# Six modulation vectors of the first layer: from TensorE to VectorE, and later in the mixer

## The chip, the core and the metric

The kernel runs on one core of a Trainium2 chip. Its metric is the device time of one execution, in microseconds. A core has TensorE (PE, with PEld for its weight loads), VectorE (DVE), ScalarE (ACT), GpSimd (POOL) and SyncE (SP), which issues the DMAs; each takes its instructions strictly in the order in which they were written for it.

## The reference, cut to what matters

Two layers run over 256 latent and 256 context tokens of width 1024. Each begins with the modulation, `mod = split(silu(c) @ w_mod + b_mod, 6)`, once for `c` and once for `c_ctx`; the two share the weights, and each of the six vectors of a layer needs a 1024x1024 matrix (4 MB in fp32). Then:

```
h  = modulate(rmsnorm(x), mod[0], mod[1])      # latent and context tokens
ys = differential attention(h), hyena convolution(h), windowed attention(h)
x  = x + mod[2] * ((sum_b sigmoid(gate_b) * (ys[b] @ w_branch[b])) @ w_out)
h2 = modulate(rmsnorm(x), mod[3], mod[4])
x  = x + mod[5] * expert_choice_moe(h2)        # router top 32 of 256 tokens, 16 experts
```

In the second layer the context tokens are only read. The vectors 2 to 5 of the first layer are thus needed at the end of its mixer at the earliest (5 only in its mixture of experts), and 0 and 1 of the second layer at that layer's start.

## The kernel before, in words

The mixer of a layer is a list of output blocks. A block is 128 columns of a projection for all 512 tokens: over eight slices k of the contraction it does three matmuls `mm3` (high and low halves of fp32 operands, so as to keep fp32 precision), 24 matmuls 128x512 into one bank. Its weights come by DMA as `wraw`; ScalarE rounds them to `wh`, and VectorE and GpSimd each form half of the rest, `wl = wraw - wh`. The first layer has 116 blocks: 0 to 23 for the eight differential heads, 24 to 47 for the hyena columns, 48 to 51 the first of the windowed attention (SWA), 52 to 107 the pairs of gate and branch for the three branches (with eight SWA blocks among the first of them), and 108 to 115 for `w_out`. Before a branch begins, the tasks whose output it reads must be finished (`drain`), and their sum is split into halves `yb`.

All else is a background task: a generator that issues a few instructions at a time between the slices k of the blocks (`Background.pump`, l. 366). Such groups are `filter` (the hyena filter), `diff` (a differential head), `hy` (a channel group of the hyena convolution: forward transform, product with `K`, inverse transform), `swa` and the modulation. Which instruction comes next is settled while the program is written down, by a cost model of the engines (`Model`, l. 144): a step is taken when its inputs are expected to be ready, a credit that grows with TensorE's time allows it, and ScalarE and VectorE aren't expected to be more than 1.5 us behind (`BACKLOG`). A group in `LAZY` stands at the end of the live tasks from when it is added, and so takes only what the others leave.

The vectors 0 and 1 of the first layer are computed before block 0. What the change touches is the rest:

- `mod_run` (l. 707) takes TensorE: for each k it loads 512 KB (`wm`, a whole row block of a vector's matrix) and issues four matmuls 32x256 in four column tiles of one bank, with both streams' `sc` as the small operand. I call these four matmuls of one k a round; a profile counts eight records for one. `mod_out` turns the result and adds the bias.
- `run` (l. 1948) adds group `modN` ahead of the mixer: vectors 2, 3, 4 of layer 0 and 0, 1 of layer 1, 40 rounds. Group `modA` is added after block 112 (l. 1555) for vector 5 of layer 0, 8 rounds, and is drained in the MoE after the first selection of tokens (l. 1887).
- `mod_vec` (l. 727) takes VectorE, and serves the second layer's vectors 3 to 5: an accumulator `ma` of 1024 columns, one operation `ma = wm * sc + ma` (scalar_tensor_tensor, STT) for each k, and at the end eight records of matmuls with a column selector, which sum over the partitions. In the second layer it is added `MODR` = 58 blocks ahead of the mixer's last.
- `pre_out` (l. 1535) drains `mod` and `modN` before block 108.

After the mixer come the routing (norm, router, selection of 32 tokens by expert) and the 16 experts, whose weights stream in by DMA.

Of the kernel before, what the change touches and what calls it, by code (L numbers as in the profile page):

```python
# [32 lines left out]
RATE = (0.75, 0.6)  # L33
LOW = (4, 3)
FAST = 1.5
COST = {"setup": 500.0, "filter": 60000.0, "mod": 15000.0, "modA": 5000.0, "modN": 5000.0, "diff": 9000.0, "hy": 10000.0, "swa": 4000.0, "post": 1000.0}
CREDIT = (3000.0, 4000.0)
SLACK = 200.0
LATER = (6, 4)
# [2 lines left out]
FILTER_E = 4  # L42
SIDE = 2
LAZY = ("mod",)
MODR = 58
PREF = ({7: 1, 6: 2, 5: 3, 4: 4}, {28: 1, 22: 2, 7: 3, 4: 4, 3: 5})
HD = 64
NH = 8
# [359 lines left out]
class Kernel:  # L408
# [295 lines left out]
        self.nc.sync.dma_start(t, self.A["w_mod"][l, k * 128:(k + 1) * 128, v * D:(v + 1) * D])  # L704
        return t

    def mod_run(self, vs, depth, pause, delay=3000.0):
        todo = [(l, v, k) for l, v in vs for k in range(KT)]
        raw = deque(self.mod_load(*todo.pop(0)) for _ in range(depth))
        yield wait(raw[0], delay=delay)  # L710
        for l, v in vs:
            acc = self.bank([128, 256], "m")
            for k in range(KT):
                w = raw.popleft()
                for c in range(4):
                    self.mm(acc[c * 32:(c + 1) * 32, :], self.sc[:, k, :], w[:, c * 256:(c + 1) * 256], k == 0, k == KT - 1, 4)
                w = None
                if todo:
                    yield wait(gate=self.room(a4=1))
                if todo:  # L720
                    raw.append(self.mod_load(*todo.pop(0)))
                yield wait(*list(raw)[:1], delay=pause)
            yield wait(acc, bank=0)
            yield from self.mod_out(l, v, acc)
            yield from self.mod_post(l, v)

    def mod_vec(self, vs):
        for l, v in vs:
            n = 2 if l == 0 or v < 2 else 1
            yield wait(gate=self.room(a4=n + 2), bank=0)  # L730
            acc = [self.sb("a4", [128, D], name="ma") for _ in range(n)]
            w = self.mod_load(l, v, 0)
            for k in range(KT):
                yield wait(w, *acc, gate=self.room(a4=1), bank=0)
                nx = self.mod_load(l, v, k + 1) if k < KT - 1 else None
                for s in range(n):
                    sc = self.sc[:, k, s:s + 1]
                    if k:
                        self.stt(acc[s], w, sc, acc[s], OP.mult, OP.add)
                    else:  # L740
                        self.ts(acc[s], w, sc, None, OP.mult)
                w, nx = nx, None
            yield wait(*acc)
            p = self.bank([128, 256], "m")
            for s in range(n):
                for c in range(4):
                    self.mm(p[c * 32:(c + 1) * 32, :], self.sel[s], acc[s][:, c * 256:(c + 1) * 256], s == 0, s == n - 1, 4)
            acc = None
            yield wait(p, bank=0)
            yield from self.mod_out(l, v, p, 30)  # L750
            yield from self.mod_post(l, v)

    def mod_post(self, l, v):
# [230 lines left out]
    def run_blocks(self, bl, ahead=2, first=3):  # L984
        nl = ns = first
        later = []
        for j, b in enumerate(bl):
            self.bg.due, end = [], self.bg.now
            for c in bl[j:]:
                if c.drains:  # L990
                    self.bg.due.append((c.drains, end))
                end += 24 * (4.0 + 0.41 * c.n)
            while ns < min(max(j + ahead, first + (j > 0)), len(bl)):
                self.split_block(bl[ns], later if j else None)
                ns += 1
            while nl < len(bl) and (nl <= ns or (nl - ns < 3 and self.model.dead("a4", BUFS["a4"]) > SPARE[self.bg.layer])):
                self.load_block(bl[nl])
                nl += 1
            if self.bg.layer and len(bl) - 1 - j == MODR:
                self.bg.add("mod", lambda task: self.mod_vec([(1, v) for v in range(3, 6)]))  # L1000
            if j < first:
                while later:
                    later.pop(0)()
                if j == 0:
                    for c in bl[:first]:
                        if c.pre:
                            c.pre()
                    hi, lo = b.hl()
                    ps = [self.bank([128, c.n], "d" if i < 2 else "b") for i, c in enumerate(bl[:first])]
                    for k in range(KT):  # L1010
                        self.bg.until([hi[:, k], lo[:, k]])
                        for c, p in zip(bl, ps):
                            self.mm3(p, (c.wh[:, k], c.wl[:, k]), (hi[:, k, 0:c.n], lo[:, k, 0:c.n]), k == 0, k == KT - 1)
                b.wh = b.wl = None
                b.evac(ps[j])
                continue
            if b.pre:
                b.pre()
            hi, lo = b.hl()[:2]
            p = self.bank([128, b.n], "d")  # L1020
            for k in range(KT):
                self.bg.until([b.wh[:, k], b.wl[:, k], hi[:, k], lo[:, k]])
                self.mm3(p, (b.wh[:, k], b.wl[:, k]), (hi[:, k, 0:b.n], lo[:, k, 0:b.n]), k == 0, k == KT - 1)
                if k >= LATER[self.bg.layer] and later:
                    later.pop(0)()
                if k > LATER[self.bg.layer] and nl < len(bl) and nl - ns < 3 and self.model.dead("a4", BUFS["a4"]) > SPARE[self.bg.layer]:
                    self.load_block(bl[nl])
                    nl += 1
                if k < KT - 1:
                    self.bg.pump()  # L1030
            b.wh = b.wl = None
            if len(bl) - 1 - j in PREF[self.bg.layer]:
                self.fill(PREF[self.bg.layer][len(bl) - 1 - j])
            b.evac(p)
            self.bg.pump()
# [335 lines left out]
    def mixer(self, l):  # L1371
# [163 lines left out]
        def pre_out():  # L1535
            halve(KT - 1)
            self.bg.drain("mod")
            self.bg.drain("modN")
            self.bg.arena = None
            self.post_start(l, nq)  # L1540

# [10 lines left out]
        for j in range(KT):  # L1552
            def ev_o(p, j=j):
# [1 line left out]
                    sl = slice(s * 256, s * 256 + 256)  # L1555
                    self.stt(self.xT[:, j, sl], p[:, sl], self.modc[l][:, 2, j, s:s + 1], self.xT[:, j, sl], OP.mult, OP.add)
                self.bg.add("post", lambda task, j=j: self.post(l, j, nq))
                if j == 4 and full:
                    vs = [(l, 5)]
                    self.bg.add("modA", lambda task: self.mod_run(vs, 2, 1300.0, 19000.0 if full else 11000.0))  # L1560
            add(cols(A["w_out"][l], j * 128), lambda: self.mg, nt, ev_o, pre_out if j == 0 else None)
        return bl

# [36 lines left out]
    def moe(self, l):  # L1600
# [61 lines left out]
        def body():  # L1662
# [221 lines left out]
            room = full  # L1884
            fill(room, 1)
            select(0)
            self.bg.drain("modA")
            fill(room, 2)
            finish(gather(0))
            for g in range(1, 4):  # L1890
# [57 lines left out]
    def run(self):  # L1948
        bl = self.mixer(0)
        self.setup(bl)  # L1950
        self.bg.add("modN", lambda task: self.mod_run([(0, 2), (0, 3), (0, 4), (1, 0), (1, 1)], 1, 6000.0))
        for l in range(L):
            if l:
                self.new_arena(3)
# [40 lines left out]
```

## Time and profile before

| | |
|---|---|
| time, three runs | 2637.61 us median, 2637.21 to 2639.09 |
| profiled execution | 2639.09 us, span 2637.3 us, so 1.8 us outside the span |
| busy in the span | PE 2244.6 (85%), DVE 1332.7 (51%), ACT 883.4 (33%), POOL 786.9 (30%) |
| chain that ended last | PE 40%, DMA 16%, DVE 13% |
| first layer's blocks start (us) | 3: 61.5; 23: 236.7; 43: 437.5; 54: 565.9; 78: 777.8; 98: 900.5; 115: 1000.2 |

The block starts are the times of each block's first matmul in the trace. By them I cut the first mixer into stretches, which the rest speaks of: A (blocks 3 to 22, 61.5 to 236.7), B (23 to 42, to 437.5), C (43 to 53, to 565.9), D1 (54 to 77, to 777.75), D2 (78 to 97, to 900.5), E (98 to 115, to 1006.9), then the routing (to 1031.3). A busy share is an average over such a stretch; what a task costs the stretch depends on which engine ends last there.

### The profile page before, as it was taken

Reading aid. Unit: us, or ns where it says so; the run is one execution under the profiler, and the core shown is the slowest. Engines: PE = TensorE matmul, PEld = TensorE weight load, DVE = VectorE, ACT = ScalarE, POOL = GpSimd, SP = SyncE. Lnnn points to the kernel's source line nnn. Section 1 sums busy time; section 2 is a strip of 40 time slices with the busy share of each in tenths; the row PEclk is TensorE's granted clock in tenths of the full one; section 3 lists DMA queues with packets and bytes.
Section 4 is the critical chain, followed back from the end, with each engine's and each line's share of the span. In section 5 each row is a group of like instructions: output and inputs, shape, how many; then the busy total and the mean of one; then the engine's idle time right before and its main releaser. Section 6 shows DMA issues by size and latency. Waiting matters only on the chain.

```text
span 2637.3 us, 38629 instructions
## 1 busy us (share of the span) xinstructions
PE 2244.6 (85%) x14938; PEld 1534.3 (58%) x14938; DVE 1332.7 (51%) x2899; ACT 883.4 (33%) x1933; POOL 786.9 (30%) x775
## 2 busy tenths in 40 slices
PE   6999998889989998898989799898888987666565
PEld 4777776767768774333333277787777863232223
DVE  4777788867662324223342158778788541111111
ACT  4445653345552332101110056553554430000001
POOL 2654225642333440001110055446554630000000
PEclk8999998989999999999999999998899988777888
DMA  8433342111213377999999942242365889999998
GB/s 293 119 120 112 96 128 89 52 53 52 69 57 88 92 251 288 373 407 400 356 379 403 404 158 80 72 121 80 100 180 160 253 308 409 409 409 409 409 409 305
DMA packets 390239, 590.31 MB, mean 224 GB/s; under 512 B 45948, under 2 KB 278056, under 8 KB 388776
## 3 DMA queue, kind: packets, MB, share of 16 engines
q1 hardware_dynamic: 390056, 587.84, 62.6%
q8 instruction: 118, 1.93, 0.3%
q14 instruction: 65, 0.53, 0.1%
HBM read 584.66 MB, written 3.15 MB: 223 GB/s over the span
## 4 chain that ended last, share of the span: by engine, by line
PE 40%; DMA 16%; DVE 13%; issue 3%; ACT 2%; SPq 2%; POOL 1%; ACTq 0%; DVEq 0%; POOLq 0%
PE p L457 38%; DMA mw<-in_moe_w_dram 15%; DVE t L260 3%; DVE arena L260 3%; PE p L468 2%; SPq L260 2%; DVE wl L260 2%; DVE qp L260 1%; DVE yb L260 1%; ACT wh L260 1%; ACT arena L260 1%; DVE ma L260 0%; DMA wraw<-in_w_in_dram 0%; DVE s L260 0%; DVE aT L260 0%
## 5 line engine op out<-in xcount | busy, mean ns | idle before, releaser
L457 PE MATMUL p<-mw,xg 128*32 128x256 f32 (+1 forms) x3072 | 406.7, 514 | 120.2 <-DMA mw<-in_moe_w_dram 120.0
L457 PE MATMUL p<-hhi,wh 128*128 128x512 f32 (+1 forms) x1344 | 496.7, 370 | 11.1 <-DVE arena L260 8.2
L457 PE MATMUL p<-hhi,wl 128*128 128x512 f32 (+1 forms) x1344 | 481.4, 358 | 26.9 <-DVE wl L260 26.4
L457 PE MATMUL p<-hlo,wh 128*128 128x512 f32 (+1 forms) x1344 | 476.6, 355 | 2.5 <-POOL hlo L260 1.4
L260 POOL TENSOR_TENSOR wl<-wraw,wh 128x512 fp32r<-128x512 f32 x232 | 330.9, 1427 | 460.2 <-ACT wh L260 365.9
L457 PEld LDWEIGHTS p<-mw,xg 128*32 128x32 f32 (+1 forms) x3072 | 137.3, 132 | 331.7 <-issue 203.7
L457 PEld LDWEIGHTS p<-hhi,wl 128*128 128x128 f32 x1344 | 258.3, 192 | 76.6 <-DVE wl L260 41.8
L457 PEld LDWEIGHTS p<-hhi,wh 128*128 128x128 f32 x1344 | 259.0, 193 | 49.3 <-issue 17.7
L457 PEld LDWEIGHTS p<-hlo,wh 128*128 128x128 f32 x1344 | 259.2, 193 | 30.3 <-POOL hlo L260 2.0
L260 ACT ACTIVATE wh<-wraw 128x1024 fp32r<-128x1024 f32 x232 | 242.1, 1053 | 43.2 <-PE p L457 12.1
L457 PE MATMUL p<-mw,aT 128*32 128x256 f32 (+3 forms) x1760 | 204.0, 483 | 59.3 <-DMA mw<-in_moe_w_dram 42.4
L260 DVE TENSOR_TENSOR wl<-wraw,wh 128x512 fp32r<-128x512 f32 x231 | 195.5, 846 | 60.1 <-ACT wh L260 58.9
L260 ACT ACTIVATE arena<-p 128x512 f32<-128x512 f32 (+1 forms) x212 | 106.0, 504 | 344.7 <-PE p L457 286.2
L260 ACT ACTIVATE yS<-p 32x256 f32<-32x256 f32 (+2 forms) x84 | 35.2, 419 | 499.3 <-PE p L457 465.8
L457 PE MATMUL p<-yb,wh 128*128 128x512 f32 (+1 forms) x768 | 197.1, 347 | 0.0
L260 POOL TENSOR_TENSOR sq<-sq,sq 128x512 f32<-128x512 f32 (+1 forms) x6 | 6.4, 1058 | 577.3 <-ACT sq L260 575.4
L457 PEld LDWEIGHTS p<-mw,aT 128*32 128x32 f32 (+1 forms) x1760 | 78.0, 134 | 167.9 <-issue 86.5
L260 DVE TENSOR_TENSOR s<-s,p 128x512 f32<-128x512 f32 (+1 forms) x32 | 17.7, 554 | 290.2 <-PE p L457 290.1
L260 DVE COPY yS<-p 32x512 f32<-32x512 f32 (+1 forms) x60 | 33.3, 556 | 244.5 <-ACT yS L260 244.5
L457 PE MATMUL p<-yb,wl 128*128 128x512 f32 (+1 forms) x384 | 133.2, 347 | 17.4 <-DVE wl L260 16.3
L457 PEld LDWEIGHTS p<-yb,wh 128*128 128x128 f32 x768 | 133.3, 195 | 15.0 <-issue 1.2
L260 ACT ACTIVATE arena<-p,t 128x512 f32<-128x512 f32 (+1 forms) x192 | 116.3, 612 | 65.2 <-DVE t L260 59.2
(235 smaller groups left out, 3506.0 us busy)
## 6 DMA issues: line engine op xcount, KB each, us to landing
mw<-in_moe_w_dram SPq DMA_DIRECT2D x173, 2048.0 KB, 19.3
wraw<-in_w_in_dram SPq DMA_DIRECT2D x152, 512.0 KB, 4.0
wm<-in_w_mod_dram SPq DMA_DIRECT2D x72, 512.0 KB, 4.5
mw<-in_moe_w_dram SPq DMA_DIRECT2D x40, 512.0 KB, 15.8
mw<-in_moe_w_dram SPq DMA_DIRECT2D x17, 1024.0 KB, 21.4
wraw<-in_w_branch_dram SPq DMA_DIRECT2D x32, 512.0 KB, 3.9
wm<-in_w_mod_dram SPq DMA_DIRECT2D x5, 2048.0 KB, 8.1
wraw<-in_w_in_dram SPq DMA_DIRECT2D x32, 256.0 KB, 3.3
```

The costliest lines, as they stand in the source:

```text
L260: return f(*args, **kw)
L457: self.nc.tensor.matmul(out, lhsT=lhsT, rhs=rhs, start=start, stop=stop, skip_group_check=tiles > 1)
L468: self.nc.tensor.transpose(out, in_, self.ident[:n, :n])
```

## The change

The six vectors of `modN` and `modA` go to one new `LAZY` task, `mod_both`, which is added 62 blocks ahead of the last one, at block 53 of the first layer. It halves the columns: for each vector and half, eight loads of 256 KB, two ahead; for each k and each of the two streams one VectorE operation of 128x512 (the first a plain product, the other seven STT), so 24 products and 168 STT in all; then four matmuls 32x256 with the selectors (48 in all). `mod_run` and the groups `modN` and `modA` go. The second layer keeps `mod_vec` and 58.

```diff
-MODR = 58
+MODR = (62, 58)
...
+    def mod_both(self, vs):
+        for l, v in vs:
+            p = None
+            for hf in range(2):
+                def load(k):
+                    t = self.sb("a2", [128, 512], name="wm")
+                    self.nc.sync.dma_start(t, self.A["w_mod"][l, k * 128:(k + 1) * 128, v * D + hf * 512:v * D + hf * 512 + 512])
+                    return t
+
+                yield wait(gate=self.room(a4=1, a2=3), bank=0)
+                acc = self.sb("a4", [128, 2, 512], name="ma")
+                ws = deque(load(k) for k in range(2))
+                for k in range(KT):
+                    yield wait(ws[0], acc, bank=0)
+                    w = ws.popleft()
+                    for s in range(2):
+                        sc = self.sc[:, k, s:s + 1]
+                        if k:
+                            self.stt(acc[:, s], w, sc, acc[:, s], OP.mult, OP.add)
+                        else:
+                            self.ts(acc[:, s], w, sc, None, OP.mult)
+                    w = None
+                    if k < KT - 2:
+                        yield wait(gate=self.room(a2=1), bank=0)
+                        ws.append(load(k + 2))
+                yield wait(acc)
+                if hf == 0:
+                    p = self.bank([128, 256], "m")
+                for s in range(2):
+                    for c in range(2):
+                        q = hf * 2 + c
+                        self.mm(p[q * 32:(q + 1) * 32, :], self.sel[s], acc[:, s, c * 256:(c + 1) * 256], s == 0, s == 1, 4)
+                acc = None
+            yield wait(p, bank=0)
+            yield from self.mod_out(l, v, p, 30)
+            p = None
             yield from self.mod_post(l, v)
...
-            if self.bg.layer and len(bl) - 1 - j == MODR:
-                self.bg.add("mod", lambda task: self.mod_vec([(1, v) for v in range(3, 6)]))
+            if len(bl) - 1 - j == MODR[self.bg.layer]:
+                vs = [(1, v) for v in range(3, 6)] if self.bg.layer else [(0, v) for v in range(2, 6)] + [(1, 0), (1, 1)]
+                self.bg.add("mod", lambda task: (self.mod_vec if self.bg.layer else self.mod_both)(vs))
...
             self.bg.drain("mod")
-            self.bg.drain("modN")
...
-                if j == 4 and full:
-                    vs = [(l, 5)]
-                    self.bg.add("modA", lambda task: self.mod_run(vs, 2, 1300.0, 19000.0 if full else 11000.0))
...
-            self.bg.drain("modA")
...
-        self.bg.add("modN", lambda task: self.mod_run([(0, 2), (0, 3), (0, 4), (1, 0), (1, 1)], 1, 6000.0))
```

Since each task's steps depend on what else is waiting, the written order moves too. Counted by blocks, before and after: the eight hyena tasks' forward transforms stand 2 in B and 6 in C, and then 5 and 3; their inverses 1 and 7, then 3 and 5. Of the 32 SWA tasks, C, D1 and D2 hold 4, 24 and 4, and then none, 22 and 10. Differential rows in A and B are 12 and 22, then 11 and 23; one of the filter's eight sections in A goes to B. The STT of the new task stand 96 in D1 and 72 in D2, its first products 14 and 10, its matmuls 24 and 24; the rounds of `modN` stood 17 in A, 21 in B and 2 in C. Behind block 115 nothing differs on any engine but the loss of `modA`.

Three places show it. The first is TensorE in block 3, where before put its first round; `p_108` is the block's bank, `wm_97` the loaded matrix rows:

```order
L457 MATMUL p_108_539<-hhi_66_337,wl_102_520 128x512
L457 MATMUL p_108_539<-hhi_66_337,wh_101_519 128x512
L457 MATMUL p_108_539<-hlo_67_338,wh_101_519 128x512
L457 MATMUL p_108_539<-hhi_66_337,wl_102_520 128x512
L457 MATMUL p_118_586<-wm_97_435,sc_22_121 32x256 x4
L468 MATMUL p_120_593<-cst_1_68,arena_10_88 128x128 x4
L457 MATMUL p_108_539<-hhi_66_337,wh_101_519 128x512
L457 MATMUL p_108_539<-hlo_67_338,wh_101_519 128x512
```

and after (the block's bank is now `p_107`):

```order
L457 MATMUL p_107_537<-hhi_66_337,wl_101_518 128x512
L457 MATMUL p_107_537<-hhi_66_337,wh_100_517 128x512
L457 MATMUL p_107_537<-hlo_67_338,wh_100_517 128x512
L457 MATMUL p_107_537<-hhi_66_337,wl_101_518 128x512
L468 MATMUL p_117_584<-cst_1_68,arena_10_88 128x128 x4
L457 MATMUL p_107_537<-hhi_66_337,wh_100_517 128x512
```

The round is gone, and the transposes of the filter task (`arena_10`) follow the block's matmuls directly. The second place is VectorE in block 64, one of the branch pairs of D1, around the `wl` of block 65 (`wl_1075` before, `wl_1003` after); `sk` and `t` with `sink` belong to SWA tasks. Before:

```order
L260 TENSOR_TENSOR wl_1055_5959<-wraw_1018_5713,wh_1054_5958 128x512
L260 STREAM_SHUFFLE sh_1072_6082<-sk_1071_6080 128x256
L260 TENSOR_TENSOR sk_1071_6080<-sk_1071_6080,cst_1_68 128x256
L260 COPY arena_117_576<-p_1073_6088 128x256
L260 COPY arena_117_576<-p_1078_6108 128x128
L260 TENSOR_TENSOR wl_1075_6092<-wraw_1034_5817,wh_1074_6091 128x512
L260 TENSOR_TENSOR wl_1082_6140<-wraw_1043_5871,wh_1081_6139 128x512
L260 SCALAR_TENSOR_TENSOR arena_9_87<-arena_9_87,p_1083_6143 128x512
```

and after:

```order
L260 TENSOR_TENSOR t_1015_5688<-t_1015_5688,nsink_82_409 128x2
L260 TENSOR_TENSOR t_1015_5688<-t_1015_5688,sink_81_408 128x2
L260 TENSOR_TENSOR qp_988_5537<-arena_114_572,qp_988_5537 64x128 x2
L260 SCALAR_TENSOR_TENSOR ma_1010_5673<-wm_1012_5676,sc_22_121,ma_1010_5673 128x512 x2
L260 TENSOR_TENSOR wl_1003_5622<-wraw_975_5466,wh_1002_5621 128x512
L260 SCALAR_TENSOR_TENSOR ma_1010_5673<-wm_1013_5680,sc_22_121,ma_1010_5673 128x512 x2
L260 COPY arena_114_572<-p_1018_5719 128x512
L260 SCALAR_TENSOR_TENSOR ma_1010_5673<-wm_1017_5717,sc_22_121,ma_1010_5673 128x512 x2
```

Between SWA's steps stand two STT of one k for each pair of rows of `ma`, directly ahead of the block's `wl` and behind it. The third place is TensorE at the end of the mixer and in the routing: `mg` with `wl` is the last block's last matmul, `xT` and `lg` are the router's, `aff` the affinities. Before:

```order
L457 MATMUL p_1430_8716<-mg_1320_7867,wl_1425_8668 128x512
L457 MATMUL p_1434_8760<-wm_1416_8614,sc_22_121 32x256 x4
L468 MATMUL p_1436_8767<-cst_1_68,xT_1371_8327 128x128 x4
L457 MATMUL p_1379_8371<-xT_1371_8327,gw_544_2974 16x256 x2
L457 MATMUL p_1434_8760<-wm_1417_8616,sc_22_121 32x256 x4
L1671 MATMUL p_1451_8816<-cst_1_68,lg_1439_8780 128x16 x2
L1671 MATMUL p_1452_8817<-cst_1_68,lg_1439_8780 128x16 x2
L457 MATMUL p_1434_8760<-wm_1435_8765,sc_22_121 32x256 x4
L457 MATMUL p_1434_8760<-wm_1454_8833,sc_22_121 32x256 x4
L457 MATMUL p_1434_8760<-wm_1455_8839,sc_22_121 32x256 x4
L457 MATMUL p_1434_8760<-wm_1456_8845,sc_22_121 32x256 x4
L457 MATMUL p_1434_8760<-wm_1457_8851,sc_22_121 32x256 x4
```

and after:

```order
L457 MATMUL p_1499_8924<-mg_1386_8053,wl_1494_8876 128x512
L468 MATMUL p_1503_8968<-cst_1_68,xT_1442_8539 128x128 x4
L457 MATMUL p_1450_8583<-xT_1442_8539,gw_1135_6446 16x256 x2
L1686 MATMUL p_1518_9013<-cst_1_68,lg_1506_8981 128x16 x2
L1686 MATMUL p_1519_9014<-cst_1_68,lg_1506_8981 128x16 x2
L468 MATMUL p_1521_9030<-cst_1_68,aff_76_403 32x128 x2
```

The rounds of `modA` stood between the router's instructions, and are gone; the router's own keep their order.

## Rows read from the trace of the kernel before

**Rows 1.** The page's second part: busy tenths in 40 slices of the span.
```profile
PE   6999998889989998898989799898888987666565
...
DVE  4777788867662324223342158778788541111111
```

**Rows 2.** Busy time by stretch: PE, PEld, DVE, ACT, POOL, clock, DMA share, GB/s.
```profile
61.50:236.70 175.20, 168.98 (x920) 126.54 (x920) 134.77 (x307) 83.83 (x184) 107.86 (x136) 1.00 0.41 120
236.70:437.50 200.80, 184.99 (x1059) 141.96 (x1058) 157.32 (x368) 105.55 (x255) 60.07 (x61) 0.97 0.36 111
437.50:565.90 128.40, 106.09 (x550) 85.47 (x549) 106.02 (x159) 53.12 (x98) 78.02 (x61) 0.91 0.18 50
565.90:777.75 211.85, 201.06 (x1173) 152.60 (x1172) 140.97 (x366) 106.34 (x258) 63.02 (x75) 0.98 0.22 60
777.75:900.50 122.75, 118.84 (x569) 96.32 (x569) 44.86 (x81) 37.39 (x64) 52.45 (x34) 1.00 0.30 87
900.50:1006.90 106.40, 106.40 (x489) 84.61 (x487) 30.33 (x50) 39.51 (x97) 42.07 (x30) 1.00 0.61 207
1006.90:1031.30 24.40, 15.93 (x192) 11.39 (x191) 17.57 (x66) 5.77 (x21) 1.15 (x1) 0.79 0.89 345
```

**Rows 3.** The same view of tile wm on PE alone: PE, clock, DMA.
```profile
61.50:236.70 175.20, 10.86 (x136) 1.00 0.41 120
236.70:437.50 200.80, 13.42 (x168) 0.97 0.36 111
437.50:565.90 128.40, 1.28 (x16) 0.91 0.18 50
```

**Rows 4.** Timeline of PE around one round: start, duration, instruction.
```profile
74.53 0.39 PE L457 MATMUL p<-hhi,wl 128*128 128x512 f32 x1
74.84 0.64 PE L457 MATMUL p<-wm,sc 128*32 128x256 f32 x8
75.41 0.50 PE L457 MATMUL p<-hhi,wh 128*128 128x512 f32 x1
```

**Rows 5.** Waits of PE in 437.5 to 565.9: total, times, longest.
```profile
PE p L457 <- DVE wl L260: 10.8, 7, 2.8
PE p L457 <- POOL yf L260: 4.8, 1, 4.8
PE p L457 <- DVE ul L260: 3.5, 3, 2.8
```

**Rows 6.** Waits of PE in 565.9 to 900.5.
```profile
PE p L457 <- DVE wl L260: 11.8, 6, 4.2
```

**Rows 7.** Groups of DVE over the whole span: busy, mean ns, idle before.
```profile
L260 DVE TENSOR_TENSOR wl<-wraw,wh 128x512 fp32r<-128x512 f32 x231 | 195.5, 846 | 60.1 <-ACT wh L260 58.9 <-DMA wraw<-in_w_branch_dram 0.3
...
L260 DVE TENSOR_SCALAR arena<-arena,t 128x512 f32<-128x512 f32 x64 | 37.2, 623 | 1.2
...
L260 DVE SCALAR_TENSOR_TENSOR ma<-wm,sc,ma 128x1024 f32<-128x1024 f32 x21 | 31.1, 1482 | 2.6 <-DMA wm<-in_w_mod_dram 2.6
...
L260 DVE SCALAR_TENSOR_TENSOR arena<-arena,t,arena 128x512 f32<-128x512 f32 x18 | 20.8, 1154 | 0.7
```

**Rows 8.** Tile ma on DVE: ns min/median/max.
```profile
L260 DVE SCALAR_TENSOR_TENSOR ma<-wm,sc,ma x21: 1269/1280/2346, 1908.1 to 2075.7; 128x1024 f32<-128x1024 f32 x21
```

**Rows 9.** A group of DVE in 437.5 to 565.9.
```profile
L260 DVE TENSOR_TENSOR arena<-arena,K 128x512 f32<-128x512 f32 x24 | 29.7, 1287 | 0.0
```

**Rows 10.** Timeline of PE in the second layer: reduction of two accumulators.
```profile
2003.85 0.64 PE L457 MATMUL p<-ma,sc 128*32 128x256 f32 x8
2004.42 0.50 PE L457 MATMUL p<-yb,wh 128*128 128x256 f32 x2
```

**Rows 11.** A group of POOL in 565.9 to 900.5.
```profile
L260 POOL TENSOR_TENSOR wl<-wraw,wh 128x512 fp32r<-128x512 f32 x44 | 62.1, 1412 | 105.9 <-ACT wh L260 72.6 <-PE p L457 12.9 <-DVE wl L260 11.2
```

**Rows 12.** Timeline of PE in the routing.
```profile
1010.19 2.37 PE L457 MATMUL p<-wm,sc 128*32 128x256 f32 x40
...
1016.46 0.58 PE L468 MATMUL p<-cst,aff 128*32 128x128 f32 x2 [3.90 <-DVE aff L260]
```

More of the change, by code (lines that the diff above doesn't have):

```diff
@@ L35 @@
 FAST = 1.5
-COST = {"setup": 500.0, "filter": 60000.0, "mod": 15000.0, "modA": 5000.0, "modN": 5000.0, "diff": 9000.0, "hy": 10000.0, "swa": 4000.0, "post": 1000.0}
+COST = {"setup": 500.0, "filter": 60000.0, "mod": 15000.0, "diff": 9000.0, "hy": 10000.0, "swa": 4000.0, "post": 1000.0}
 CREDIT = (3000.0, 4000.0)
@@ L705, in mod_load @@
         return t
[L707 to L725, printed above, removed]
     def mod_vec(self, vs):
@@ L750, in mod_vec @@
             yield from self.mod_out(l, v, p, 30)
+            yield from self.mod_post(l, v)
+    def mod_both(self, vs):
[33 more added lines that the diff above has]
+            p = None
             yield from self.mod_post(l, v)
```

## The prediction

> **What bounds the kernel now.** I read the page's slices first [rows 1]: TensorE shows nine tenths through most of the first mixer, and VectorE falls from seven or eight tenths to two or four in the later part. The trace cut by block starts says it sharply [rows 2]. TensorE's idle time is the stretch less its first figure: 6.2 us in A, 15.8 in B, 22.3 in C, 10.8 in D1, 3.9 in D2 and none in E. VectorE's share is 77%, 78%, 83%, 67%, 37% and 29%. So A, D2 and E end with TensorE's work, and an instruction taken from it there is time gained. B and C hold real waiting: in C TensorE waits 10.8 us for `wl` of VectorE, 4.8 for `yf` of GpSimd and 3.5 for `ul` of VectorE, 19.1 of the 22.3 [rows 5]. VectorE's room lies in D1 (71 us) and above all D2 (78) and E (76) [rows 2]. The granted clock is 0.91 in C and 0.97 to 1.00 elsewhere in the mixer; I don't count on a change of it.
>
> **What a round costs.** The rounds in A, B and C have 136, 168 and 16 records, eight to a round: 17, 21 and 2 [rows 3]. Around one of them two block matmuls start at 74.53 and 75.41, 0.88 us apart [rows 4]; the step without a round is about 0.23 (the round itself starts 0.31 after the first and takes 0.57 to the next). So a round displaces 0.65 us, a little more than the 0.08 a record of its own busy time.
>
> **Prices of tasks.** A block takes 24 x 0.23 = 5.5 us of TensorE. D1 runs 24 blocks and 24 SWA tasks: (201.1 - 24 x 5.5) / 24 = 2.9 us of TensorE a task at most, of which I take 2.2, since D1's transposes and scores of unfinished pairs are in it; VectorE: (141.0 - 24 x 0.85 for `wl` [rows 7]) / 24 = 5.0 at most, and I take 4.5. C runs 11 blocks, 6 forward and 7 inverse hyena transforms, 4 SWA tasks and 2 rounds: TensorE (106.1 - 60.5 - 8.8 - 1.3) / 6.5 = 5.5 a hyena task, VectorE (106.0 - 9.4 - 18) / 6.5 = 12.1 [rows 2, 3].
>
> **Stretch A.** 17 rounds x 0.65 = 11.1 us leave an engine that is busy 169.0 of 175.2. Besides, one of eight filter sections and one of twelve differential rows move to B; what A holds beside blocks and rounds is 169.0 - 110 - 10.9 = 48 us for these twenty pieces, 2.4 each, so 5 more. Together -16, with nothing late in their place that the trace shows; -11 if the moved pieces were hidden.
>
> **Stretch B.** 21 rounds x 0.65 = 13.7 leave TensorE, the two pieces (+5) and 2.5 hyena tasks (3 forward, 2 inverse; +13.8) come: 185.0 becomes 190. VectorE gets 2.5 x 12.1 = 30 and about 4 for the row: 157 becomes 191 of the present 200.8. So VectorE becomes what B ends with; I take +4, 204.8. Ends: -10 if the 30 us fill VectorE's 43 us of idle time without a wait, +14 if its share stays below 90% (191 / 0.89).
>
> **Stretch C.** It loses 2 rounds (1.3), 4 SWA tasks (8.8) and 2.5 hyena tasks (13.8) on TensorE: 106.1 becomes 82. VectorE loses 18 + 30 and falls to 58, so most of the wait for `wl` and `ul` should go; what stays is the last inverse transforms and the split to `yb` that begin branch 0. I leave 13 us of idle time for it, of 22.3: 95 instead of 128.4, -33. Ends: -14 (the transforms' share comes back as waiting, since they follow each other through VectorE and GpSimd), -38 (only 8 us idle).
>
> **Stretches D1 and D2.** TensorE first. The 24 small matmuls in each end six halves; eight such records take 0.57 us [rows 10], and a half with four, with the turn of the result, I put at 1 us. D1: 201.1 - 2 x 2.2 + 6 = 203. D2: 118.8 + 6 SWA tasks x 2.2 + 6 = 138. VectorE then. Before has no STT of this shape. From below: half of the shortest 1024-column one, 1.269 / 2 = 0.635 us [rows 8]. From above: a 128x512 STT of three operands with two tiles from SBUF, mean 1.154 [rows 7]. Nearest is the same operation on twice the columns, mean 1.482, half 0.74 [rows 7]; I stay near it, a fifth of the way to the upper end: 0.82. The first products go by 0.623 [rows 7]. D1: 141.0 - 9 + 96 x 0.82 + 14 x 0.62 = 219. D2: 44.9 + 27 + 72 x 0.82 + 10 x 0.62 = 137. So in D1 VectorE passes TensorE, and in D2 they are level. No instruction waits for an accumulation until its half is complete, so it can fill gaps, and I let VectorE be 96% busy in D1: 228, +16. D2 I let end with TensorE's 138 and its present 4 us of idle time, 143, +20. Ends for both together: +20 (0.635: D1 then ends with TensorE, 203 + 10.8), +95 (1.154 at the same shares).
>
> What is queued behind an STT is `wl` of the next block, whose lateness costs TensorE already 11.8 us in these stretches [rows 6]; a pair of STT ahead of it makes it up to 1.6 us later, and that is what the idle shares above hold. The loads are 96 of 256 KB on SP, in stretches whose DMA share is 0.22 and 0.30 [rows 2]; before, they were 48 of 512 KB, the same bytes. I charge nothing; were the weights' loads held up behind them on SP, `wraw` has the three blocks that are loaded ahead for cover.
>
> **Stretch E and the routing.** E's list doesn't change but for `modA`'s first round. In the routing the rounds lie in idle time: 40 records run from 1010.19, while TensorE has nothing else until 1016.46 and then still waits 3.90 us for `aff` of VectorE [rows 12]. So 0.2 us leave with the turning of the result. Behind it the experts' weights stream, and all shifts together.
>
> **The sum.** -16 + 4 - 33 + 16 + 20 - 0.2 = -9.2 us. Against the profiled execution, 2639.1 (span 2637.3 and 1.8 around it), that is 2629.9; against the median of the runs, 2637.6, it is 2628.4. I say 2629.
>
> **Rivals.** First, slower: VectorE and GpSimd hold each other up in D1 and D2. The same STT in the second layer takes between 1.269 and 2.346 us [rows 8], the product with `K` in C 1.287 on average [rows 9] at the new STT's 512 columns; GpSimd's busy share is 61% in C and 30% and 43% in D1 and D2 [rows 2], and its `wl` take 1.412 each [rows 11]. If an STT that meets one of these waits for the rest of it, 0.7 us on average, with a chance of 0.36, it takes 0.635 + 0.25 = 0.89, and with GpSimd's own halves of `wl` coming later by as much, 0.95 to 1.0. At 1.0 D1 is (140.7 + 96) / 0.96 = 247 and D2 (78 + 72) / 0.97 = 155, +67 instead of +36: 2660. It decides from about 0.88 us an STT on, where D1 and D2 have eaten the whole gain (45 us). Against it: the second layer's mean is only 1.17 of its least, beside a GpSimd as busy.
> The Trainium skill has a rule for this ("SBUF — State Buffer", section on the two separate sides): an operation of VectorE with two inputs in SBUF and one of GpSimd that reads SBUF share a port pair as an exclusive lock, and whichever starts first keeps it for the whole instruction. The trace agrees in that the longest STT exceeds the shortest by 1.077 us, less than one GpSimd `wl` [rows 8, 11]. By the rule alone the time would be about 2640 from the 0.89 above, and more where GpSimd waits in turn.
>
> Second, no change: C keeps its waits. The last hyena tasks end in a chain of inverse transforms and of the split, one behind the other, and the 4.8 us wait for `yf` [rows 5] is of that kind. C gains only 14 to 20 and B is at +8: 2629 + 15 + 4 is 2648 at the worst, and about 2640 in the middle. For it speaks that five of eight inverses are still in C; against it that VectorE's load there is halved.
>
> Third, a larger gain: the accumulations really are filler, at 0.7 us, and VectorE's halves of `wl` get by. Then D1 is +6, D2 +17, and the time 2616.
>
> **Chances.** The forecast 0.45, with its own range 2619 to 2636; the larger gain 0.15; no change 0.18; VectorE and GpSimd in each other's way 0.22. What a measurement of this kernel can tell from no change is about 0.2%, 5.3 us, so between 2632.3 and 2642.9 counts as the same. Faster: 0.15 + 0.37 of the forecast's; same: its other 0.08 and 0.16 of the second; slower: 0.22 and 0.02. The range is 2606 to 2658: below it lies only a larger gain with B's good end, above it an STT of 1.0 and more.
>
> **What would show it.** In the profile after: no `wm` on TensorE in the first mixer; block 23 starts 16 us earlier, block 43 12, block 54 45, block 78 29, block 98 and the routing 9 earlier. The group of STT `ma` 128x512 has 168 entries with a mean near 0.82; VectorE's busy share in D1 is about 96%, and TensorE's wait for `wl` there not much over 20 us. I am wrong if block 54 starts less than 30 us earlier (C's term), or if the STT's mean is 0.9 or more and the gain of block 54 is gone by block 98 (D's).

## The result, and the profile after

The changed kernel takes 2659.47 us (median of 4 runs) against 2638.35 for the kernel before: a ratio of 1.0074, 95% interval 1.0062 to 1.0086. It is slower by about 20 us, where I had forecast 9 faster. My first rival's price, 2660, is the time measured, but by luck: it was made of 67 us more in D1 and D2, which grew by 45.

The profiled execution has a span of 2658.8 us, 21.5 more than before. The stretches, cut at the starts of the same blocks as in [rows 2], with the same columns:

```profile
62.50:220.40 157.90, 150.04 (x751) 121.46 (x751) 117.71 (x267) 78.41 (x168) 100.81 (x127) 1.00 0.26 74
220.40:437.10 216.70, 186.50 (x961) 154.22 (x960) 186.02 (x423) 117.74 (x285) 80.44 (x81) 0.93 0.18 53
437.10:534.40 97.30, 82.61 (x398) 67.53 (x398) 74.15 (x89) 40.49 (x65) 65.90 (x52) 0.93 0.23 60
534.40:753.60 219.20, 205.56 (x1144) 152.61 (x1142) 199.97 (x438) 92.23 (x221) 62.41 (x64) 0.98 0.42 123
753.60:914.30 160.70, 149.88 (x793) 110.90 (x791) 142.12 (x258) 54.92 (x119) 58.67 (x43) 0.99 0.44 135
914.30:1020.80 106.50, 106.50 (x489) 84.69 (x488) 30.34 (x50) 39.52 (x97) 42.10 (x30) 1.00 0.56 188
1020.80:1045.20 24.40, 11.12 (x124) 9.25 (x123) 17.16 (x63) 5.72 (x21) 1.15 (x2) 0.72 0.67 259
```

Read down the first figure of each row: A is 17.3 us shorter than before, B 15.9 longer, C 31.1 shorter, D1 7.3 and D2 38.0 longer, E and the routing as they were. Over A to D2 that is 839.0 us before and 851.8 after. TensorE's busy time in it, the second figure, fell only from 780.0 to 774.6, and its idle time rose from 59.0 to 77.2. VectorE's busy time rose by 136 us, and in D1 and D2 it is now busy 342 of 380.

The new group's price, by the view of VectorE's groups, in D1:

```profile
L260 DVE SCALAR_TENSOR_TENSOR ma<-wm,sc,ma 128x512 f32<-128x512 f32 x94 | 74.8, 838 | 0.2
```

and in D2 (busy us, then mean ns of one):

```profile
L260 DVE SCALAR_TENSOR_TENSOR ma<-wm,sc,ma 128x512 f32<-128x512 f32 x74 | 71.4, 1015 | 0.1
```

Over both the mean of one is 0.916 us. (These are cut by time; by the blocks in which they are written it is 96 and 72.) What TensorE waits for in D1 and D2, to be read against [rows 6]:

```profile
PE p L457 <- DVE wl L260: 17.7, 16, 3.6
PE p L468 <- DVE arena L260: 2.5, 7, 0.6
```

The same wait as before, 11.8 us in 6 pieces, has become 17.7 in 16. Here is one of them, seen on three engines. VectorE (the first two rows are the two STT of one k):

```profile
817.71 0.75 DVE L260 SCALAR_TENSOR_TENSOR ma<-wm,sc,ma 128x512 f32<-128x512 f32 x1
818.38 1.76 DVE L260 SCALAR_TENSOR_TENSOR ma<-wm,sc,ma 128x512 f32<-128x512 f32 x1
820.06 0.68 DVE L260 TENSOR_TENSOR wl<-wraw,wh 128x512 fp32r<-128x512 f32 x1
...
822.17 1.41 DVE L260 SCALAR_TENSOR_TENSOR ma<-wm,sc,ma 128x512 f32<-128x512 f32 x2
```

GpSimd at the same time:

```profile
818.33 1.26 POOL L260 TENSOR_TENSOR wl<-wraw,wh 128x512 fp32r<-128x512 f32 x1 [2.38 <-ACT arena L260]
```

and TensorE:

```profile
817.65 0.71 PE L457 MATMUL p<-yb,wh 128*128 128x512 f32 x2
820.79 0.50 PE L457 MATMUL p<-yb,wl 128*128 128x512 f32 x1 [2.43 <-DVE wl L260]
```

The first STT was under way when GpSimd's `wl` started at 818.33, and takes 0.75 us. The second started 0.05 us after GpSimd and takes 1.76: it ends at 820.14, 0.55 us after GpSimd's operation. The pair takes 2.43 us in all; the next pair, with nothing beside it, 1.41. VectorE's own half of `wl` stands behind the first pair, and TensorE waits 2.43 us for it.

In the routing the rounds' removal shows as idle time that grew, in answer to [rows 12]:

```profile
1030.39 0.58 PE L468 MATMUL p<-cst,aff 128*32 128x128 f32 x2 [6.20 <-DVE aff L260]
```

The wait for `aff` is 6.20 instead of 3.90 us, and nothing is gained: from the start of block 115 to the next layer's first block it is 544.0 us in the changed kernel and 544.1 before.

### The profile page after: what moved, and what is told of

Same layout as the page of the kernel before. It is cut to its first block, busy times and chain, and to the rows that moved or that the text cites. A ratio compares the mean times of both kernels' runs of the same rounds, so it can differ in the third digit from the quotient of the medians.

```text
span 2658.8 us, 38353 instructions
## 1 busy us (share of the span) xinstructions
PE 2233.6 (84%) x14650; PEld 1538.3 (58%) x14650; DVE 1471.4 (55%) x3091; ACT 880.3 (33%) x1933; POOL 792.9 (30%) x775
## 4 chain that ended last, share of the span: by engine, by line
PE 42%; DVE 28%; DMA 18%; issue 5%; ACT 4%; POOL 2%; SPq 1%; DVEq 0%; ACTq 0%; POOLq 0%
PE p L457 40%; DMA mw<-in_moe_w_dram 16%; DVE arena L260 7%; DVE t L260 6%; DVE ma L260 5%; DVE wl L260 3%; PE p L468 2%; DVE qp L260 2%; DMA wm<-in_w_mod_dram 1%; ACT arena L260 1%; SPq L260 1%; DVE yc L260 1%; DVE yb L260 1%; ACT wh L260 1%; POOL arena L260 1%
## 5 line engine op out<-in xcount | busy, mean ns | idle before, releaser
L457 PEld LDWEIGHTS p<-hlo,wh 128*128 128x128 f32 x1344 | 260.3, 194 | 31.1 <-POOL hlo L260 1.9
L260 DVE TENSOR_TENSOR wl<-wraw,wh 128x512 fp32r<-128x512 f32 x231 | 194.1, 841 | 20.6 <-ACT wh L260 18.9
L260 DVE SCALAR_TENSOR_TENSOR ma<-wm,sc,ma 128x512 f32<-128x512 f32 (+1 forms) x189 | 179.6, 991 | 4.1 <-DMA wm<-in_w_mod_dram 3.8
L260 DVE TENSOR_TENSOR s<-s,p 128x512 f32<-128x512 f32 (+1 forms) x32 | 17.7, 554 | 289.5 <-PE p L457 289.3
## 6 DMA issues: line engine op xcount, KB each, us to landing
mw<-in_moe_w_dram SPq DMA_DIRECT2D x40, 512.0 KB, 14.7
mw<-in_moe_w_dram SPq DMA_DIRECT2D x17, 1024.0 KB, 21.5
```

The lines of the kernel that those rows point to most:

```text
L260: return f(*args, **kw)
L457: self.nc.tensor.matmul(out, lhsT=lhsT, rhs=rhs, start=start, stop=stop, skip_group_check=tiles > 1)
```

## The experiments

The table gives for each run the profiled execution's blocks 3 to 97 (A to D2), TensorE's busy time in them, D1 and D2 together, all that lies behind block 98, and the timed median with its ratio to the kernel before on the same chip.

| run | blocks 3-97 | PE busy | D1+D2 | behind 98 | median | ratio (95%) |
|---|---|---|---|---|---|---|
| before | 839.0 | 780.0 | 334.6 | 1736.8 | 2638.35 | |
| after | 851.8 | 774.6 | 379.9 | 1744.5 | 2659.47 | 1.0074 (1.0062-1.0086) |
| e1 one k | 832.5 | 765.8 | 360.2 | 1740.7 | 2637.29 | 0.9998 (0.9982-1.0013) |
| e2 seat held | 863.8 | 782.3 | 386.9 | 1746.7 | 2674.53 | 1.0142 (1.0121-1.0163) |
| e3 begin at 73 | 843.9 | 766.8 | 372.4 | 1779.1 | 2684.12 | 1.0177 (1.0156-1.0198) |
| e4 free seat | 834.3 | 779.4 | 342.8 | 1734.9 | 2635.00 | 0.9985 (0.9968-1.0002) |
| e5 short STT | 826.8 | 766.1 | 355.1 | 1742.6 | 2636.44 | 0.9998 (0.9988-1.0007) |
| e6 no GpSimd wl | 828.4 | 765.2 | 359.3 | 1746.1 | 2643.23 | 1.0019 (1.0004-1.0034) |
| e7 lazy rounds | 829.4 | 771.8 | 342.3 | 1738.3 | 2637.80 | 0.9998 (0.9986-1.0011) |
| e8 nothing | 822.1 | 753.7 | 339.7 | 1734.3 | 2622.15 | 0.9943 (0.9920-0.9965) |
| e9 writes only | 832.5 | 769.3 | 361.0 | 1746.7 | 2637.89 | 0.9997 (0.9980-1.0014) |
| e10 VectorE all wl | 845.3 | 772.9 | 372.6 | 1741.4 | 2650.84 | 1.0058 (1.0038-1.0077) |
| e11 before, no GpSimd wl | 832.4 | 780.0 | 327.9 | 1738.2 | 2631.68 | 0.9972 (0.9957-0.9988) |
| e12 before, VectorE all wl | 829.0 | 777.6 | 325.2 | 1740.9 | 2634.24 | 0.9980 (0.9971-0.9990) |

Each row's first four figures are those of one execution; the four timed runs of the changed kernel alone lie 9.0 us apart, so a few us in one place are not a finding by themselves.

My first theories were that VectorE's load in D is the price (V), that TensorE's own additional work there is (T), and that the place a modulation task had taken among the four live tasks explains B and C (S). From e6 on it is that GpSimd's reading beside the STT is the price (G, then P), or that its halves of `wl` come late (L).

**e1, one k.** The STT are left out:

```diff
-                ws = deque(load(k) for k in range(2))
-                for k in range(KT):
+                ws = deque(load(k) for k in range(1))
+                for k in range(1):
```

> The changed kernel with seven of the eight k of each accumulation left out, and their loads: the 24 first products and the 48 small matmuls stay, the 168 STT go. Up to block 53 its order is that of the changed kernel. If the STT are what makes D1 and D2 long (theory V), blocks 54 to 97 fall from 380 us to about 350 (before has 335, but four SWA tasks less in them and no reductions), and the time is about 2630. If TensorE's additional SWA tasks and reductions make them long (theory T), they stay at 370 or more and the time at 2650 or more. Block 54 starts 31 us earlier than before by both.

D is 360.2, between the two, and so is the time. Of the 45 us by which D had grown, 20 go with the STT. The other 25 are TensorE's: D1 and D2 hold 12 us of reductions and the four SWA tasks that C had lost. Even with the STT for nothing the change would be worth nothing that can be measured.

**e2, seat held.** In blocks 24 to 42 one task fewer is live:

```diff
-... < WIDTH[self.layer] and
+... < WIDTH[self.layer] - self.held and
```

> The changed kernel with one task fewer live at a time in blocks 24 to 42, as when a modulation task took one of the four places there. Its hyena tasks stand 2 and 6 in B and C, as in the kernel before. Theory S (the place that became free pulls hyena tasks into B, and B's wait comes from that): B is 187 to 190 us instead of 217, C 120 to 127 instead of 97, so block 54 starts within 5 us of the changed kernel's, and with three SWA tasks in C again D is 8 to 10 us shorter: about 2650. Theory R (B's waits come from the order without rounds as such): B stays above 210 and the time is 2659 or more.

B went to 197.8 and C to 119.6, the way that S says, though B is 8 us above its range: B's added length is what C lost. But B and C together are 317.4 against 314.0, D is 7 us longer instead of 8 to 10 shorter, and the time rose by 15 instead of falling by 9. So the free place explains where the hyena tasks stand, and isn't the harm.

**e3, a later begin.** `MODR = (42, 58)` instead of `(62, 58)`.

> The changed kernel with the new task added 42 instead of 62 blocks ahead of the last one, at block 73: 14 STT stand in D1, 96 in D2, 58 in E, whose VectorE was busy 30 of 106 us. Theory V (VectorE's total in D1 and D2 is the bound, and room later is free): D1 about 223, D2 145 to 150, E 106 to 110, which sum up to 474 to 483 against 486 in the changed kernel: 2647 to 2656. If STT cost TensorE nothing where VectorE has idle time, D2 128 and E 107: 2632. If each STT disturbs the blocks' own wl wherever it stands, the sum is as long as in the changed kernel: 2660.

A miss for all three. D fell by 7.5 us to 372.4, but the task wasn't through when `w_out` began: block 107 with the drain behind it took 27.2 us instead of 5.4. TensorE's waits from 967.0 to 1001.6:

```profile
PE p L457 <- DVE ma L260: 16.9, 2, 8.8
```

**e4, free seat with the rounds kept.** The count of live tasks leaves out `modN`:

```diff
-... t.group not in LAZY for t in self.live) < WIDTH
+... t.group not in LAZY and t.group != "modN" for t in self.live) < WIDTH
```

> The kernel before, with its 40 rounds on TensorE, but the modulation task not counted among the four live tasks: 6 and 2 forward hyena transforms stand in B and C, and all SWA tasks behind C. Theory S: B is about 20 us longer than before, C 30 shorter, D longer by the four SWA tasks, 12 us: the time about that of before, 2638 to 2641. If the fourth task were a gain in itself, C's 30 us would stay: 2615 to 2625.

A +4.3, B +22.1, C -39.3, D +8.2 us against before: the shift of hyena and SWA tasks comes from the place alone, with every round still on TensorE, and pays for itself within 5 us. The time, 2635.0, lies between the two expectations, and its interval holds no difference.

**e5, short STT.** Same place for every instruction, less time in these 168:

```diff
-self.stt(acc[:, s], w, sc, acc[:, s], OP.mult, OP.add)
+self.model.op("DVE", [acc[:, s]], [w, sc, acc[:, s]], 66.0 + 1.042 * 512 + 60.0)
+self.nc.vector.eng.scalar_tensor_tensor(out=acc[:, s, 0:32], in0=w[:, 0:32], scalar=sc, in1=acc[:, s, 0:32], op0=OP.mult, op1=OP.add)
```

> The changed kernel with every instruction of every engine in the same place, but each of the 168 STT works on 32 columns instead of 512, which leaves out most of the sums. Blocks 3 to 97 took 839.0 us before, 851.8 in the changed kernel, 832.5 with one k. If VectorE's time in the STT is the price (theory V), D1 and D2 together fall from 380 to 360 or less, and the time is 2636 to 2641. If the written order is the price (theory O: SWA tasks pushed from D1 into D2 because the planner believed VectorE to be busy), D stays at 372 or more and the time at 2652 or more.

D is 355.1: theory V. With the order untouched, 25 us are the time that the STT take on VectorE. The short ones still wait for GpSimd: their mean is 0.386 us, where those with nothing beside them take 0.244, 24 us in all. So with VectorE busy 259 of 355 us such waits cost little: D is 5 us shorter than e1's, which has no STT at all.

**e6, GpSimd without its wl.** V alone doesn't say why 146 us in an engine that was half idle should cost 25. In the same order again:

```diff
-self.tt(b.wl[:, c:], b.raw[:, c:], h[:, c:], OP.subtract, self.nc.gpsimd)
+self.nc.gpsimd.eng.memset(b.wl[:, c:].bitcast(F32), 0.0)
```

> The changed kernel in the same order, but GpSimd's halves of wl for the blocks split from block 53 on are set to zero (an operation that reads nothing) in place of the difference, which leaves that part out. If VectorE's STT wait for GpSimd's reading (theory G), their mean falls from 0.870 to 0.78 or less in both D1 and D2, and D is 8 us or more shorter. If not, the mean stays at 0.84 or more, and D within 4 us of 380.

D is 359.3, 20.6 us shorter with the STT at full length: nearly all of the price. So the price is no sum of two parts: e5 and e6 each take most of it away, and it arises where both are there, GpSimd's reading and a VectorE that is nearly full (342 of 380 us; here 314 of 359). The expected 0.870 and 0.78 were busy time for one STT; it fell to 0.760 (127.8 us for 168). The mean of a record, which overlaps with the next one's, fell from 0.916 to 0.805.

**e7, lazy rounds.** `LAZY = ("mod", "modN")` in the kernel before.

> The kernel before, with its 40 rounds on TensorE, but their task at the end of the live ones from the start, so that it takes what the others leave and no place among the four. The rounds stand 18 in A and 22 in B, the hyena tasks 6 and 2. If a place taken by a modulation task cost before anything (theory S'), it is 4 to 8 us faster than before: 2632 to 2636. If the 5 us by which the kernel with the free place was ahead were chance: 2638 to 2642.

No difference: e4's 5 us were not a gain of the place. (Block 3 starts at 68.0 us here and at 61.0 to 65.5 in the others, with a round ahead of it, so its 829.4 are not quite comparable.)

**e8, nothing instead.** `mod_both` sets its six vectors to a constant.

> The changed kernel with the six vectors left out altogether (constants in their place): no rounds, no STT, no reductions. It bounds what any removal of the rounds can bring. If TensorE's work decides (theory T), blocks 3 to 97 take 26 us less than before, 813, and 13 less than with one k, for the 48 small matmuls: 2618 to 2625. If the waits of B and D1 take it back: 825 or more, 2630 or more.

The median is as theory T has it, 2622, though the blocks take 822.1 and not 813. TensorE's busy time fell by 26.3 us, the rounds' price; 9.4 came back as idle time. Against e1 it shows the reductions' price: 12.1 us busy.

**e9, GpSimd writes only.** In e6 GpSimd was quicker too. Here the memset runs three times:

```diff
+for _ in range(3):
+    self.nc.gpsimd.eng.memset(b.wl[:, c:].bitcast(F32), 0.0)
```

> As the run in which GpSimd's halves of wl were set to zero, in the same order, but each by three such operations in a row (0.54 us each), so that GpSimd is occupied for about as long as by the real subtraction (1.53 us) and finishes its half as late, without reading anything. If its reading at the same time as VectorE is the price (theory P), D stays short, 359 to 366, and the STT's mean near 0.81. If GpSimd's late halves are the price, through whoever waits for them (theory L), D goes back to 374 to 380.

D is 361.0 and the time 2637.9: theory P. GpSimd was as busy as in the changed kernel, 123 us in D against 121, and D is within 2 us of e6's. TensorE's wait for `wl` in D1 and D2, 17.7 us in the changed kernel, is half of that:

```profile
PE p L458 <- DVE wl L260: 8.5, 9, 3.2
```

VectorE in e9:

```profile
559.99 1.41 DVE L260 SCALAR_TENSOR_TENSOR ma<-wm,sc,ma 128x512 f32<-128x512 f32 x2
```

beside GpSimd in e9:

```profile
559.70 1.70 POOL L990 MEMSET wl<- 128x512 f32 x3 [5.47 <-PE p L458]
```

The pair lies wholly inside GpSimd's 1.70 us and takes what a pair takes alone. Its group of STT in D1 and D2:

```profile
L260 DVE SCALAR_TENSOR_TENSOR ma<-wm,sc,ma 128x512 f32<-128x512 f32 x168 | 129.8, 818 | 2.1 <-DMA wm<-in_w_mod_dram 1.8
```

Sorted by what GpSimd did beside them, the 168 STT of the changed kernel fall apart. 119 overlap no operation of GpSimd that reads: 0.745 us on average. 49 overlap one, and their mean, 1.332, is again a mean of two cases. 16 of them had started before GpSimd's operation: 0.739 to 0.752. 31 started while it ran: 1.185 to 1.829, on average 1.672, and each ends 0.547 to 0.553 us after GpSimd's. The last two started in its final 0.08 us, and take 0.745. GpSimd waits in turn: seven of its sums `arena` started about 0.16 us after an STT, and each ends 1.14 to 1.15 us after that STT. In e9, 13 STT started while a reading operation (`arena`, `yb`, `sk`, `kl`) ran: 1.220 to 1.783; 50 overlap a memset alone: 0.742; 97 nothing: 0.745.

**e10, VectorE forms all of wl in D.** A complete kernel:

```diff
+        if self.late_blocks:
+            c = KT
+        else:
+            self.tt(b.wl[:, c:], b.raw[:, c:], h[:, c:], OP.subtract, self.nc.gpsimd)
```

> A complete kernel: the changed one, with the whole of wl on VectorE, and none on GpSimd, for the blocks split from block 53 on. VectorE gets about 44 x 0.65 = 29 us more work in D. By theory P the conflict goes, and the STT's mean falls to 0.81 or less; D is 360 to 372 and the time 2642 to 2652. By theory V (VectorE's load alone) D is longer than 380 and the time 2660 to 2675.

D is 372.6 and the STT's mean 0.811; both a hair above theory P's ends, and far from theory V's 380. D is 7 us shorter than in the changed kernel, though VectorE's `wl` take 54.6 us there instead of 33.0. By the medians 9 us come back, by the ratios 4, and the two intervals overlap; it isn't enough to catch the kernel before.

**e11, before without GpSimd's wl.** The edit of e6 on the kernel before.

> The kernel before, in its own order, with GpSimd's halves of wl set to zero for the blocks split from block 53 on, as in the run on the changed kernel. It prices the same edit where no STT run. Theory P: the 21 us it gave in the changed kernel came from the STT's company, so here D (334.6 us) gets 2 to 8 us shorter. If GpSimd's halves hold up the blocks anyway, it gets 15 us shorter or more, and the comparison of the two kernels loses its meaning.

D is 6.7 us shorter. So of the 19 to 21 us that GpSimd's reading costs in the changed kernel's D, about 7 were there before, and 12 to 14 came with the STT.

**e12, before with all of wl on VectorE.** The edit of e10 on the kernel before.

> A complete kernel that may beat both: the kernel before, with its rounds on TensorE, and the whole of wl on VectorE for the blocks split from block 53 on, where VectorE has room (186 us busy of 335 in D, plus some 29). By theory P the conflict with GpSimd, worth 7 us in this kernel where GpSimd only wrote zeros, goes, and a part of it is paid back by the longer wl (1.24 us in one piece instead of two halves side by side): D 328 to 333, the time 2 to 6 us below the kernel before. If the longer wl is late for its block, D is 335 to 345 and the time the same or up to 8 us more.

D is 325.2 us, and the time 0.9980 of the kernel before (0.9971 to 0.9990): it beats both, by about 4 and 25 us. VectorE forms the whole of `wl` in 58.0 us for 44, where it had room:

```profile
L260 DVE TENSOR_TENSOR wl<-wraw,wh 128x1024 fp32r<-128x1024 f32 x44 | 58.0, 1321 | 36.7 <-ACT wh L260 36.5
```

It also answers a doubt on e6, e9 and e11, which give TensorE zeros for half of `wl`: here the data are whole, and D is 9.4 us shorter, more than e11's 6.7.

## Why the prediction was wrong

**What held.** The rounds' price (26 us of TensorE by 40 x 0.65; e8: 26.3), the reductions' (12 us; 12.1), A (-16; -17.3), and the routing (nothing). C's size held too (-33; -31.1), but not its reason: I had most of the wait for `wl` go and the last inverse transforms stay. The wait for `ul` went, that for `yf` fell from 4.8 to 1.9 us, and that for `wl` rose from 10.8 [rows 5] to 12.7 of C's 14.7 us of idle time, so the size is luck in part:

```profile
PE p L457 <- DVE wl L260: 12.7, 5, 5.4
```

**The step that failed** is the price of an STT and what I made of it: "Nearest is the same operation on twice the columns ... 0.82", and "I let VectorE be 96% busy in D1". The mean is 0.916, past the 0.88 from which I had the first rival decide. That rival had the cause right and its parts wrong: 0.36 of the STT waiting 0.7 us, on top of 0.635, where 0.18 of them (31 of 168) wait 0.93 on top of 0.745. The mean hides two prices: 0.745 for an STT that starts before or away from GpSimd's reading, and 1.672 on average for one that starts in the middle of it; 31 x 0.93 = 29 us of VectorE's 146 are waiting. I had both in view, 1.269 and 2.346 in [rows 8], and averaged them into one number, as if the excess were spread over all. It isn't: 17 of the 31 stand beside GpSimd's `wl`, the other 14 beside its sums `arena` and `yb` and one `sk`, and VectorE's half of `wl` is formed at about the same moment, from the same `wh`. In four of the 16 pieces of TensorE's wait, 9.2 of the 17.7 us, an STT that waited stands among the four instructions ahead of that `wl`; by which way the rest of the price reaches TensorE is not shown. The rule that I quoted from the Trainium skill ("SBUF — State Buffer", the two separate sides), an exclusive lock for the whole instruction between a two-input operation of VectorE and a reading one of GpSimd, agrees with the trace: the one that started first takes 0.739 to 0.752 us, the one that came second ends 0.55 us after the other, and beside an operation that only writes it is 0.742.

With the STT at the price that I had forecast (e9: mean 0.818) blocks 3 to 97 are 6.5 us shorter than before, near my 9; with GpSimd's reading they are 12.8 longer. So this step turned the mixer's gain into a loss. It isn't the whole miss: forecast and span lie 30.7 us apart, of which 11.9 are B's, 9.3 those of D1 and D2 together, 7.7 lie behind block 98, and 1.8 elsewhere.

**D in total** grew by 45.3 us, not 36: 7.3 in D1 and 38.0 in D2, where I had 16 and 20. Only 9 of the price's 19 to 21 us show in that difference, since the rest of D was priced too high: without the reading D grows by 26.4 (e9). D2 alone was sized too low even so: TensorE's work in it is 145.6 us in e9, where I had 138. VectorE was busy 91% of D1 and 88% of D2, never the 96% I let it have; with SWA's steps and `wl` in one queue, TensorE waits before that.

**B** was sized at +4, its bad end at +14, and it is +15.9. It has no STT, and e8 has the same 216 us, so this is order: the hyena tasks moved in. TensorE's work there is 186.5 us, less than the 190 I had, and VectorE's 186.0 is 86% of B, so neither fills it: TensorE's idle time doubled, from 15.8 to 30.2. The granted clock fell too, from 0.97 to 0.93, which I hadn't counted on; what of B it makes is not shown. e2 and e4 show that such a shift is handed back by C. I had added up C's gain at nearly its full size and B's loss at a fraction. Over B and C TensorE's busy time fell by 22.0, and its idle time rose by 6.8: 15 us gained where my terms made it 29.

**Behind block 98** the span is 7.7 us longer, where I had "all shifts together". That is the second step that failed. Nothing is written differently there but the routing. 4.5 of it lie behind the second mixer, where the last expert's matmuls wait 3.7 us for nothing that the profile shows ("issue"), in before and then in after:

```profile
L457 PE MATMUL p<-mw,aT 128*32 128x64 f32 x256 | 4.2, 220 | 1.4 <-DMA mw<-in_moe_w_dram 0.9 <-DVE aT L260 0.5
```

```profile
L457 PE MATMUL p<-mw,aT 128*32 128x64 f32 x256 | 5.4, 244 | 4.3 <-issue 3.7 <-DVE aT L260 0.5
```

The runs with the whole new task (e2, e5, e6, e9, e10) all take 498 to 500 us behind the second mixer, and those without it or with one k (before, e1, e4, e7, e8, e11, e12) 493 to 495. But e3, which has the whole task too, only later, takes 493.7. That "issue" time is 1.6 to 3.7 us in those that take 498 to 500, and at most 0.2 in the others. So it isn't the task as such; what brings it, the runs leave open. The other 3 us lie in the second layer's mixer, which takes 597.9 to 605.1 us over the 14 kernels. From the start of block 115 to the second layer's first block, the same before and after, it is 544.0 to 550.1 over all of them, for a reason that is open too. By such terms e5, e6 and e9, whose blocks 3 to 97 are 6 to 12 us shorter than before, are not faster at the end: behind block 98 they take 5.8 to 9.9 us more.

**The account** of blocks 3 to 97, from 839.0: rounds away, -26.3 of TensorE's work and +9.4 of idle time (e8, 822.1); reductions, first products and 168 short STT, +4.7 (e5, 826.8); STT at full length with GpSimd's `wl` not reading, +1.6 to +5.7 (e6, e9); GpSimd's reading beside them, +19.3 to +23.4 (851.8). The last two steps hold in this order only: in e5 GpSimd reads as in the changed kernel, D is the shortest of the four, and the full length then costs 25.0.

## What to carry to other kernels

An idle share of an engine is not a price list: before moving work onto VectorE, look up which of its neighbours on GpSimd read at the same time, and which instruction stands behind it in the queue; a mean duration over both cases hides exactly what decides. Work taken off one stretch by a planner turns up in another, so add up the busy time of the bounding engine over all of them, and count as gain only what leaves the sum. Forty rounds of small matmuls that cost 26 us of TensorE were cheap beside 146 us of VectorE and 12 of reductions.

## What was unexpected in the hardware

Whether an STT waits is settled by who starts first, to within some hundredths of a us. An STT of 128x512 takes 0.745 us beside nothing, 0.742 beside a memset of GpSimd, and 0.739 to 0.752 when a reading operation of GpSimd starts after it. When it starts after that operation, it ends 0.547 to 0.553 us behind it, whether it came early (1.829 us) or late (1.185). The mean over all that overlap, 1.332, describes neither case. With 32 columns (e5) the shortest takes 0.234 us, with 512 0.734; but one with 32 that comes second still takes up to 1.375, and ends 0.046 to 0.053 us behind GpSimd's operation.
